# When a two-block transformer kernel takes the result tiles of its seven-product pairs and asks its residual back

## The chip, the cores and the metric

The kernel runs on one core of a Trainium2 chip. The metric is the device time of one execution in microseconds (us); the time of a kernel is the median of its runs.

## The reference

Two transformer blocks run one after the other on 512 tokens of width 1024, in float32. The change touches only the two feed-forward parts (FFNs) of the second block, which are the same code with other weights:

```
def swiglu(h, w_gate, w_up, w_down):
    return (jax.nn.silu(h @ w_gate) * (h @ w_up)) @ w_down
...
x = x + 0.5 * swiglu(rms_norm(x, ffn1_norm), ffn1_w_gate, ffn1_w_up, ffn1_w_down)
x = x + hybrid_mixer(x, ...)
x = x + 0.5 * swiglu(rms_norm(x, ffn2_norm), ffn2_w_gate, ffn2_w_up, ffn2_w_down)
return rms_norm(x, final_norm)
```

The hidden width is 2816, which is 22 pairs of 128 gate columns and 128 up columns.

## The kernel before, in words

Activations lie with the features on the 128 partitions and the 512 tokens along the free dimension; the residual is eight such tiles, `x[0]` to `x[7]`. Every float32 product is made of three fast passes: each operand is split into a rounded high part and the remaining low part, and the kernel multiplies high by high, high by low and low by high. For weights, a tile `raw` lands by DMA, ScalarE casts it to `whi` (line 364, `copy`), and VectorE subtracts to get `wlo` (line 374, `tt`). There are six buffers each for `raw`, `whi` and `wlo`, so a cast waits until TensorE has done with an earlier tile.

One FFN is the function `swiglu`. Its 22 pairs are made in three parts of 4, 9 and 9 (`PARTS`). After each part, the down product of that part's pairs is added into the residual: four groups, each for two residual tiles, with `d_evac` adding each finished accumulator into `x` on VectorE (line 370, `stt`). The four pairs of the first part are plain products on `xgh`/`xgl`. The 18 pairs of the other two parts are made with seven products of half size in place of eight (`CHAINS`, in the order p1, p5, u, p2, v, c12, c21). They need combinations of the normalized input, the forms: tiles `b1`, `b2`, `c` and `d`, made by `make_forms` on VectorE for four slices `kk` and split into `fh` (ScalarE) and `fl` (VectorE). The first chain, p1, reads `b11` for kk 0 to 3, then p5 reads `t1`, u reads `t2` (from `c`), and so on.

When the seven products of a pair are done, `seven_evac` hands the pair to a background generator, `seven_end`: Silu of the gate tile `e` on ScalarE (line 360, `act`), two multiplies on VectorE with the up tile, then the split into `hidh` (ScalarE) and `hidl` (VectorE, line 370). The down product reads `hidh` and `hidl`; a pair whose tiles are not yet made is waited for by `hidget`.

All these activation tiles come from one pool of 61 slots (`SLOTS`, function `T2`). The residual does not fit there all the time. So `first` (before part one) and `away` (after parts one and two) store the eight tiles in DRAM (`xs_f1`, `xs_f2`), and `back` loads them again: before the change in one go of eight loads, in part one ahead of the first down group, in the other parts ahead of the last pair. All loads and stores are issued by one queue, SP, in program order.

The order on each engine is fixed when the program is built. The main loop `run_units` writes TensorE's products out, and after every few of them calls `beside`, which may add one weight step and then polls the background lanes (class `Lanes`). A lane may take its next step only if `room(lane)` says that slots are left (for a lane that has begun: at most `SLOTS - 2` in use), if a planner (`Plan`) with a cost for each instruction thinks the inputs ready, and if it thinks VectorE and ScalarE not too far behind TensorE. A step that isn't allowed stays where it is until a later poll, or until the product that needs it forces it. Engines run their own rows strictly in that order.

Of the kernel before, what the change touches and what calls it, by code (L numbers as in the profile page):

```python
# [146 lines left out]
def bare(a):  # L147
    return a.ap if isinstance(a, View) else a
# [93 lines left out]
def tile_two_blocks(  # L242
# [43 lines left out]
    def committed():  # L286
        return live[0] + sum(max(0, bg.lanes[i][0][1] - bg.lanes[i][0][2][0]) for i in bg.want)

    def room(lane):
        if lane in bg.want:  # L290
            return live[0] <= SLOTS - 2
        return committed() + bg.lanes[lane][0][1] <= SLOTS - SPARE
# [7 lines left out]
    bg = Lanes(plan, len(SLACK), banks_free, room)  # L300

    def T2(name, shape=(P, T), dt=F32):
        return View(t2p.tile(list(shape), dt, name=name, tag="t2"), Token(live, bg.owner))
# [58 lines left out]
    def copy(out, in_):  # L362
        plan.op("ACT", 130.0 + width(out) / 1.2, [out], [in_])
        nc.scalar.copy(bare(out), bare(in_))  # L364
# [7 lines left out]
    def tt(out, in0, in1, op):  # L372
        plan.op("DVE", 100.0 + width(out) * 1.04, [out], [in0, in1])
        nc.vector.tensor_tensor(out=bare(out), in0=bare(in0), in1=bare(in1), op=op)  # L374
# [39 lines left out]
    def load(out, in_):  # L414
        n = 1
        for d in out.shape:
            n *= d
        plan.op("DMA", n * 4 / 360.0, [out], [], wait=2000.0)
        nc.sync.dma_start(out=bare(out), in_=bare(in_))
# [38 lines left out]
    def pair(name):  # L458
        return T2(name + "h", dt=F32R), T2(name + "l", dt=F32R)
# [5 lines left out]
    def split(src, name):  # L465
        hi, lo = pair(name)
        split_to(hi, lo, src)
        return hi, lo
# [65 lines left out]
    def add_group(*a, **k):  # L534

        g = Group(*a, **k)
        base = state["total"]
        count = len(g.pairs)
        t = 0.0
        if g.kind == "kout":  # L540
            for k in range(g.kt):
                units.append({"g": g, "k0": k, "kn": KU, "need": base + t})
                t += KU * 1360.0
            state["total"] = base + t
            return g
        if g.kind == "seven":
            for part, at in enumerate((0.0, 1.0, 3.0, 5.0)):
                units.append({"g": g, "pi": 0, "part": part, "kn": KU, "need": base + at * SEVENTH})
            state["total"] = base + 7.0 * SEVENTH
            return g  # L550
        for k0 in range(0, g.kt, g.ku):
            kn = min(g.ku, g.kt - k0)
            for pi in range(count):
                need = {
                    "feat": t + (pi * 1360.0 if count > 1 else 0.0),
                    "tok": k0 * 680.0,
                    "half": (2 * pi * g.kt + k0) * 360.0,
                    "halfin": (k0 * count + pi * kn) * 720.0,
                }[g.kind]
                units.append({"g": g, "pi": pi, "k0": k0, "kn": kn, "need": base + need})  # L560
            t += kn * count * (2720.0 if g.kind == "tok" else 1360.0)
        state["total"] = base + t
        return g
# [240 lines left out]
    x = [None] * 8  # L804
# [349 lines left out]
    hid = {}  # L1154
# [17 lines left out]
    xget = lambda k, cs=None: xg[k]  # L1172
# [16 lines left out]
    for hf in range(2):  # L1189
        i0 = 12 * hf  # L1190
        for i in range(i0, i0 + 12):
            if i == 0:
                add_group([ffn_up[0], ffn_up[1]], 8, h2get, up_evac(0),
                          kind="halfin")
            elif i > 1:
                add_group([ffn_up[i]], 8, h2get, up_evac(i), post=h.clear if i == 23 else None)
        for pp in range(4):
            add_group([ffn_down[pp][:, i0:i0 + 12, :]], 12, lambda k, cs=None, i0=i0: hid[i0 + k], dn_evac(pp, hf == 1),
                      post=hid.clear if pp == 3 else None)
# [8 lines left out]
    def drop(name, tiles):  # L1208
        rn.pop(name, None)
        tiles.clear()  # L1210

    def rnorm(name):
        bg.until(lambda: name in rn)
        return rn[name]
# [42 lines left out]
    def swiglu(wgu, wd, hidden, rname, gname, pre, d_last):  # L1257
        def gu_evac(i0):
            def ev(pi, j, ps):
                i = i0 + pi  # L1260
                r = rnorm(rname)
                if j == 0:
                    t = T2("sg")
                    tt(t, ps, r, ALU.mult)
                    act(t, t, AF.Silu)
                    tt(t, t, r, ALU.mult)
                    half[i] = t
                else:
                    t = half.pop(i)
                    tt(t, t, ps, ALU.mult)  # L1270
                    hidden[i] = split(t, "hid")
            return ev

        def seven_evac(i):
            got = {}
            L, R = slice(0, HALF), slice(HALF, T)

            def ev(what, ps):
                if what == "p1":
                    got["e"] = T2("e")  # L1280
                    copy(got["e"][:, L], ps)
                elif what == "p5":
                    got["o"] = T2("o")
                    copy(got["o"][:, R], ps)
                elif what == "u":
                    copy(got["e"][:, R], ps)
                elif what == "p2":
                    e = got["e"]
                    tt(e[:, L], ps, e[:, L], ALU.add)
                elif what == "v":  # L1290
                    copy(got["o"][:, L], ps)
                elif what == "c12":
                    e, o = got["e"], got["o"]
                    tt(e[:, R], ps, e[:, R], ALU.add)
                    tt(o[:, R], o[:, L], o[:, R], ALU.add)
                else:
                    bg.add(seven_end(i, got.pop("e"), got.pop("o"), ps), 0, 2)
            return ev

        def seven_end(i, e, o, ps):  # L1300
            L, R = slice(0, HALF), slice(HALF, T)
            yield (e,), 0
            act(e, e, AF.Silu)
            yield (e,), 0
            tt(e[:, R], e[:, R], o[:, R], ALU.mult)
            yield (e, ps), 0
            tt(e[:, L], e[:, L], ps, ALU.mult)
            del ps, o
            yield (e,), 0
            hi, lo = pair("hid")  # L1310
            act(hi, e, AF.Copy, scale=-1.0)
            yield (hi,), 0
            stt(lo, e, -1.0, hi.bitcast(F32), ALU.mult, ALU.subtract)
            hidden[i] = hi, lo

        def d_evac(pp, last):
            def ev(pi, j, ps, cs=ALL):
                if j is not None:
                    m = 2 * pp + j
                    stt(x[m][:, cs], ps[:, cs], 0.5, x[m][:, cs], ALU.mult, ALU.add)  # L1320
                if last:
                    d_last(pp, j, cs)
            return ev

        saved = {}

        def save():
            xd = saved["x"] = dram.tile([8, P, T], F32, name="xs_" + rname)
            for f in range(8):
                store(xd[f], x[f])  # L1330

        def first():
            save()
            pre()
            bg.add(make_forms(gname, rname, dict(enumerate(x))), 4, 6)
            x[:] = [None] * 8

        def back():
            for f in range(8):
                x[f] = T2("x")  # L1340
                load(x[f], saved["x"][f])

        def away():
            hidden.clear()
            save()
            x[:] = [None] * 8

        def plain_done():
            bg.until(lambda: "r" in forms)
            drop(rname, xg)  # L1350

        def hidget(i0):
            def get(k, cs=None):
                bg.until(lambda: i0 + k in hidden)
                return hidden[i0 + k]
            return get

        i0 = 0
        for n in PARTS:
            last = i0 + n == 22  # L1360
            if i0 == 0:
                add_group([wgu[0], wgu[1]], 8, xget, gu_evac(0), pre=first)
                for i in range(2, n):
                    add_group([wgu[i]], 8, xget, gu_evac(i), post=plain_done if i == n - 1 else None)
            else:
                for i in range(i0, i0 + n):
                    add_group([wgu[i]], 8, formget, seven_evac(i), kind="seven", pre=back if i == i0 + n - 1 else None,
                              post=forms.clear if i == 21 else None)
            for pp in range(4):
                kind = "half" if (last and pp == 3 and rname == "f2") else "feat"  # L1370
                post = None if pp < 3 else hidden.clear if last else away
                add_group([wd[pp][:, i0:i0 + n, :]], n, hidget(i0), d_evac(pp, last), kind=kind,
                          pre=back if i0 == 0 and pp == 0 else None, post=post)
            i0 += n

    def f1_pre():
# [347 lines left out]
    for what in MIX_ORDER.split():  # L1724
        b, evac = pieces[what[0]]
        pp = int(what[1])
# [282 lines left out]
```

## Time and profile before

| | |
|---|---|
| time, median of 3 runs | 1889.35 us (1888.68 to 1891.15) |
| the profiled execution | 1887.91 us, of which the span of the trace is 1886.1 us |
| TensorE busy | 1850.1 us, 98% of the span |
| VectorE busy | 1288.6 us, 68% |
| ScalarE busy | 961.3 us, 51% |
| chain of work that ended last | TensorE 91%, VectorE 5%, ScalarE 2%, DMA 1% |
| mean granted TensorE clock | 0.995 of full speed |

PE is TensorE, PEld its weight load (which runs beside PE), DVE is VectorE, ACT is ScalarE, SPq the queue of SP that issues DMAs. In a timeline, a row is: start in us from the span's start, duration in us, engine, line and operation, output<-input, partitions x elements, how many instructions were merged; in brackets, how long the engine had been idle before and what ended that. A matmul's duration is its time in the pipeline, so the pace of TensorE is read from the starts. In a table of stretches, a row is: the stretch, its length, the busy us of PE, PEld, DVE, ACT and POOL (instructions in brackets), the granted TensorE clock (1.00 is 2.4 GHz, 0.50 is 1.2 GHz), the DMA engines' share and GB/s. Buffer numbers are left out of names in the trace.

### The profile page before, as it was taken

To read this page: it belongs to the slowest core of one execution; us is meant where nothing else is said; L and a number is where in the kernel's file an instruction comes from. 1 tells how busy PE (TensorE), PEld (TensorE's weight loads), DVE (VectorE), ACT (ScalarE), POOL (GpSimd) and SP (SyncE) were. 2 spreads that over 40 slices of the span, in tenths; PEclk is the share of its full clock that TensorE was granted. 3 is DMA by queue.
4 is the path that set the end of the run, shared out by engine and by line. 5 is a ranking of instruction groups with operands and counts; after the bars stand their busy time and mean duration, and the time that the engine had idled before them with its cause. 6 is when DMAs were issued, how large, how long until landed. Compare 5 with 4: busy or idle time off the path is not lost.

```text
span 1886.1 us, 25909 instructions
## 1 busy us (share of the span) xinstructions
PE 1850.1 (98%) x10046; PEld 1571.5 (83%) x10046; DVE 1288.6 (68%) x2120; ACT 961.3 (51%) x1512; POOL 28.0 (1%) x53
## 2 busy tenths in 40 slices
PE   9999999999999999999999999999999999999997
PEld 6878777789888888888997998788777788988996
DVE  8799876656764466558883784677845778955864
ACT  6778686635442244343552463454576443542552
POOL 0000000000000000000000000211000000000000
PEclk9999999999999999999999999999999999999999
DMA  9665521241333323343343335321223234353341
GB/s 355 202 209 166 165 82 66 80 139 53 112 111 104 97 89 102 100 136 101 123 128 130 125 115 175 134 90 56 80 68 123 80 121 166 94 177 102 111 157 45
DMA packets 90880, 229.55 MB, mean 122 GB/s; under 512 B 10754, under 2 KB 23170, under 8 KB 90756
## 3 DMA queue, kind: packets, MB, share of 16 engines
q1 hardware_dynamic: 90756, 227.89, 36.7%
q8 instruction: 79, 1.29, 0.3%
q14 instruction: 45, 0.37, 0.1%
HBM read 211.07 MB, written 16.78 MB: 121 GB/s over the span
## 4 chain that ended last, share of the span: by engine, by line
PE 91%; DVE 5%; ACT 2%; DMA 1%; issue 1%; SPq 0%; DVEq 0%; POOLq 0%; ACTq 0%
PE acc L328 83%; PE z L328 1%; PE av L328 1%; PE pt L337 1%; DVE wlo L374 1%; DVE x L370 1%; DVE cc L370 1%; ACT whi L364 0%; DMA x<-in_xT_dram 0%; PE pd L328 0%; PE hms L328 0%; PE pg L328 0%; PE nms L328 0%; PE pe L328 0%; PE psr L328 0%
## 5 line engine op out<-in xcount | busy, mean ns | idle before, releaser
L374 DVE TENSOR_TENSOR wlo<-raw,whi 128x1024 fp32r<-128x1024 f32 (+2 forms) x396 | 445.2, 1140 | 204.7 <-ACT whi L364 201.6
L364 ACT CAST whi<-raw 128x1024 fp32r<-128x1024 f32 (+2 forms) x396 | 386.2, 985 | 325.3 <-PE acc L328 237.9
L328 PE MATMUL acc<-hh,whi 128*128 128x512 f32 (+1 forms) x800 | 298.7, 385 | 1.4 <-ACT hh L360 1.4
L328 PE MATMUL acc<-hl,whi 128*128 128x512 f32 (+1 forms) x800 | 295.6, 381 | 0.2 <-DVE hl L370 0.2
L328 PE MATMUL acc<-hh,wlo 128*128 128x512 f32 (+1 forms) x800 | 295.7, 381 | 0.0
L328 PE MATMUL acc<-fl,whi 128*128 128x256 f32 x1008 | 286.2, 284 | 4.5 <-DVE fl L374 4.5
L328 PE MATMUL acc<-fh,whi 128*128 128x256 f32 x1008 | 286.1, 284 | 0.4 <-ACT fh L364 0.4
L328 PE MATMUL acc<-fh,wlo 128*128 128x256 f32 x1008 | 285.9, 284 | 0.0
L328 PE MATMUL acc<-hidh,whi 128*128 128x512 f32 (+1 forms) x562 | 216.7, 386 | 7.9 <-ACT hidh L360 7.1
L328 PE MATMUL acc<-hidl,whi 128*128 128x512 f32 (+1 forms) x562 | 216.6, 385 | 0.9 <-DVE hidl L370 0.4
L328 PE MATMUL acc<-hidh,wlo 128*128 128x512 f32 (+1 forms) x562 | 216.1, 385 | 0.0
L328 PEld LDWEIGHTS acc<-fl,whi 128*128 128x128 f32 x1008 | 194.3, 193 | 5.0 <-DVE fl L374 4.9
L328 PEld LDWEIGHTS acc<-fh,whi 128*128 128x128 f32 x1008 | 194.2, 193 | 0.8 <-ACT fh L364 0.6
L328 PEld LDWEIGHTS acc<-fh,wlo 128*128 128x128 f32 x1008 | 194.2, 193 | 0.0
L328 PEld LDWEIGHTS acc<-hh,whi 128*128 128x128 f32 x800 | 150.3, 188 | 32.6 <-issue 2.3
L328 PEld LDWEIGHTS acc<-hh,wlo 128*128 128x128 f32 x800 | 150.4, 188 | 29.0
L328 PEld LDWEIGHTS acc<-hl,whi 128*128 128x128 f32 x800 | 150.6, 188 | 28.1 <-DVE hl L370 0.4
L328 PE MATMUL acc<-xgh,whi 128*128 128x512 f32 x352 | 142.9, 406 | 1.8 <-DVE x L370 1.8
L328 PE MATMUL acc<-xgh,wlo 128*128 128x512 f32 x352 | 137.4, 390 | 0.0
L328 PE MATMUL acc<-xgl,whi 128*128 128x512 f32 x352 | 137.2, 390 | 0.0
L328 PEld LDWEIGHTS acc<-hidh,whi 128*128 128x128 f32 x562 | 106.4, 189 | 30.2 <-ACT hidh L360 8.0
L328 PEld LDWEIGHTS acc<-hidl,whi 128*128 128x128 f32 x562 | 106.4, 189 | 22.6 <-DVE hidl L370 1.1
(301 smaller groups left out, 2679.0 us busy)
## 6 DMA issues: line engine op xcount, KB each, us to landing
raw<-in_w_in_dram SPq DMA_DIRECT2D x68, 512.0 KB, 4.2
adt<-in_ada_wT_dram SPq DMA_DIRECT2D x96, 256.0 KB, 5.5
raw<-in_ffn_up_dram SPq DMA_DIRECT2D x48, 512.0 KB, 3.8
raw<-in_f1gu_dram SPq DMA_DIRECT2D x44, 512.0 KB, 3.8
raw<-in_f2gu_dram SPq DMA_DIRECT2D x44, 512.0 KB, 3.8
raw<-in_ffn_down_dram SPq DMA_DIRECT2D x24, 512.0 KB, 4.3
xs_f<-x SPq DMA_DIRECT2D x48, 256.0 KB, 4.6
x<-xs_f SPq DMA_DIRECT2D x48, 256.0 KB, 5.6
```

Source lines behind the costliest of these rows:

```text
L328: nc.tensor.matmul(bare(out), bare(w), bare(x), start=start, stop=stop, **kw)
L337: nc.tensor.transpose(bare(out), bare(in_), idt)
L364: nc.scalar.copy(bare(out), bare(in_))
L370: nc.vector.scalar_tensor_tensor(out=bare(out), in0=bare(in0), scalar=bare(scalar), in1=bare(in1), op0=op0, op1=op1, **kw)
L374: nc.vector.tensor_tensor(out=bare(out), in0=bare(in0), in1=bare(in1), op=op)
```

## The change

Three edits. `seven_evac` takes the two result tiles `hi` and `lo` when it hands the pair over, and `seven_end` no longer asks for any: it is added with a need of 0, and `room` lets a lane whose generator needs 0 pass always. `back` takes the tiles to load: in parts two and three, `x[0]` to `x[3]` are loaded ahead of the last pair, as all eight were, and `x[4]` to `x[7]` ahead of the first down group. In part one, all eight are now loaded ahead of the last gate/up pair, one pair earlier than before.

```
--- before.py
+++ after.py
@@ -287,6 +287,8 @@
         return live[0] + sum(max(0, bg.lanes[i][0][1] - bg.lanes[i][0][2][0]) for i in bg.want)
 
     def room(lane):
+        if bg.lanes[lane][0][1] == 0:
+            return True
         if lane in bg.want:
             return live[0] <= SLOTS - 2
         return committed() + bg.lanes[lane][0][1] <= SLOTS - SPARE
@@ -1294,10 +1296,10 @@
                     tt(e[:, R], ps, e[:, R], ALU.add)
                     tt(o[:, R], o[:, L], o[:, R], ALU.add)
                 else:
-                    bg.add(seven_end(i, got.pop("e"), got.pop("o"), ps), 0, 2)
+                    bg.add(seven_end(i, got.pop("e"), got.pop("o"), ps, *pair("hid")), 0, 0)
             return ev
 
-        def seven_end(i, e, o, ps):
+        def seven_end(i, e, o, ps, hi, lo):
             L, R = slice(0, HALF), slice(HALF, T)
             yield (e,), 0
             act(e, e, AF.Silu)
@@ -1307,7 +1309,6 @@
             tt(e[:, L], e[:, L], ps, ALU.mult)
             del ps, o
             yield (e,), 0
-            hi, lo = pair("hid")
             act(hi, e, AF.Copy, scale=-1.0)
             yield (hi,), 0
             stt(lo, e, -1.0, hi.bitcast(F32), ALU.mult, ALU.subtract)
@@ -1335,10 +1336,12 @@
             bg.add(make_forms(gname, rname, dict(enumerate(x))), 4, 6)
             x[:] = [None] * 8
 
-        def back():
-            for f in range(8):
-                x[f] = T2("x")
-                load(x[f], saved["x"][f])
+        def back(fs):
+            def pre():
+                for f in fs:
+                    x[f] = T2("x")
+                    load(x[f], saved["x"][f])
+            return pre
 
         def away():
             hidden.clear()
@@ -1361,16 +1364,17 @@
             if i0 == 0:
                 add_group([wgu[0], wgu[1]], 8, xget, gu_evac(0), pre=first)
                 for i in range(2, n):
-                    add_group([wgu[i]], 8, xget, gu_evac(i), post=plain_done if i == n - 1 else None)
+                    end = i == n - 1
+                    add_group([wgu[i]], 8, xget, gu_evac(i), pre=back(range(8)) if end else None, post=plain_done if end else None)
             else:
                 for i in range(i0, i0 + n):
-                    add_group([wgu[i]], 8, formget, seven_evac(i), kind="seven", pre=back if i == i0 + n - 1 else None,
+                    add_group([wgu[i]], 8, formget, seven_evac(i), kind="seven", pre=back(range(4)) if i == i0 + n - 1 else None,
                               post=forms.clear if i == 21 else None)
             for pp in range(4):
                 kind = "half" if (last and pp == 3 and rname == "f2") else "feat"
                 post = None if pp < 3 else hidden.clear if last else away
                 add_group([wd[pp][:, i0:i0 + n, :]], n, hidget(i0), d_evac(pp, last), kind=kind,
-                          pre=back if i0 == 0 and pp == 0 else None, post=post)
+                          pre=back(range(4, 8)) if i0 and pp == 0 else None, post=post)
             i0 += n
 
     def f1_pre():
```

No instruction is added or removed in either FFN; TensorE's rows are the same in the same order. What moves stands in the same way in both FFNs at the end of part two, and in slightly different ways at the start of it. Line numbers above 290 are two higher after the change.

ScalarE, first FFN, end of part two: the last pair's gate tile is `e_8451` before and `e_8445` after; `raw_8417` and `raw_8463` before (`raw_8419` and `raw_8457` after) are the weight tiles of the third down group. Before:

```order
L364 COPY o_8471<-acc_8437 128x256
L364 CAST whi_8524<-raw_8318 128x1024
L364 CAST whi_8540<-raw_8371 128x1024
L364 CAST whi_8558<-raw_8407 128x256
L364 CAST whi_8594<-raw_8417 128x1024
L364 CAST whi_8624<-raw_8463 128x1024
L360 ACTIVATE e_8451<-e_8451 128x512
L360 ACTIVATE hidh_8632<-e_8451 128x512
```

After the change:

```order
L366 COPY o_8465<-acc_8431 128x256
L366 CAST whi_8516<-raw_8320 128x1024
L366 CAST whi_8532<-raw_8371 128x1024
L366 CAST whi_8552<-raw_8407 128x256
L362 ACTIVATE e_8445<-e_8445 128x512
L362 ACTIVATE hidh_8550<-e_8445 128x512
L366 CAST whi_8601<-raw_8419 128x1024
L366 CAST whi_8631<-raw_8457 128x1024
```

The Silu and the cast that makes `hidh` have moved ahead of two weight casts. On VectorE the two multiplies and the subtraction that makes `hidl` move ahead of the two matching `wlo` rows in the same way.

VectorE, first FFN, the last rows before the first seven-product pair reads the forms of its last slice (`b1_7245`, `b2_7246`, `c_7247`, `d_7143` before; `b1_7231`, `b2_7232`, `c_7233`, `d_7159` after). `x_...<-acc` is a residual tile that takes up a down product, `raw<-raw` are the sums of weights that the seven products need. Before:

```order
L370 SCALAR_TENSOR_TENSOR x_7203<-acc_7332,x_7203 128x512
L374 TENSOR_TENSOR c_7247<-b2_7246,b1_7245 128x256
L374 TENSOR_TENSOR b1_7245<-b1_7245 128x256
L370 SCALAR_TENSOR_TENSOR c_7247<-b1_7245,b2_7246 128x256
L370 SCALAR_TENSOR_TENSOR d_7143<-c_7247,b2_7246 128x256
L370 SCALAR_TENSOR_TENSOR x_7205<-acc_7346,x_7205 128x512
L374 TENSOR_TENSOR wlo_7366<-raw_7168,whi_7364 128x1024
L374 TENSOR_TENSOR wlo_7388<-raw_7190,whi_7386 128x1024
L374 TENSOR_TENSOR fl_7395<-b1_7245,fh_7393 128x512
L374 TENSOR_TENSOR fl_7405<-b2_7246,fh_7397 128x512
L374 TENSOR_TENSOR fl_7424<-c_7247,fh_7407 128x512
L374 TENSOR_TENSOR fl_7443<-d_7143,fh_7426 128x512
```

After the change, the making of `c` and `d` stands some 20 rows further up, with that of `b1` and `b2`:

```order
L372 SCALAR_TENSOR_TENSOR b1_7231<-x_3621,vec_78,nr_6855 128x512
L372 SCALAR_TENSOR_TENSOR b2_7232<-x_3629,vec_78,nr_6855 128x512
L376 TENSOR_TENSOR c_7233<-b2_7232,b1_7231 128x256
L376 TENSOR_TENSOR b1_7231<-b1_7231 128x256
L372 SCALAR_TENSOR_TENSOR c_7233<-b1_7231,b2_7232 128x256
L372 SCALAR_TENSOR_TENSOR d_7159<-c_7233,b2_7232 128x256
L372 SCALAR_TENSOR_TENSOR x_7100<-acc_7225,x_7100 128x512
```

and where the rows of before stood, there are now:

```order
L376 TENSOR_TENSOR fl_7341<-b1_7231,fh_7336 128x512
L376 TENSOR_TENSOR raw_7206<-raw_7184,raw_7293 128x4x128
L376 TENSOR_TENSOR raw_7206<-raw_7184 128x4x128
L376 TENSOR_TENSOR raw_7184<-raw_7206,raw_7184 128x4x128
L376 TENSOR_TENSOR raw_7302<-raw_7184,raw_7293 128x4x128
L372 SCALAR_TENSOR_TENSOR x_7110<-acc_7332,x_7110 128x512
L376 TENSOR_TENSOR fl_7366<-b2_7232,fh_7343 128x512
L372 SCALAR_TENSOR_TENSOR x_7112<-acc_7356,x_7112 128x512
L376 TENSOR_TENSOR wlo_7376<-raw_7184,whi_7374 128x1024
L376 TENSOR_TENSOR wlo_7398<-raw_7206,whi_7396 128x1024
L376 TENSOR_TENSOR fl_7424<-c_7233,fh_7368 128x512
L376 TENSOR_TENSOR fl_7443<-d_7159,fh_7426 128x512
```

The making of `c` and `d` has moved up, to before the second residual tile; `fl` of `b1` and `b2` has moved ahead of the two `wlo` rows; `fl` of `c` and `d` still stands behind them.

VectorE, second FFN, the same place. Before:

```order
L370 SCALAR_TENSOR_TENSOR x_13656<-acc_13789,x_13656 128x512
L370 SCALAR_TENSOR_TENSOR x_13658<-acc_13803,x_13658 128x512
L374 TENSOR_TENSOR wlo_13821<-raw_13615,whi_13819 128x1024
L374 TENSOR_TENSOR wlo_13843<-raw_13643,whi_13841 128x1024
L374 TENSOR_TENSOR fl_13848<-b1_13711,fh_13813 128x512
L374 TENSOR_TENSOR fl_13858<-b2_13712,fh_13850 128x512
L374 TENSOR_TENSOR fl_13877<-c_13713,fh_13860 128x512
L374 TENSOR_TENSOR fl_13896<-d_13587,fh_13879 128x512
```

After the change:

```order
L372 SCALAR_TENSOR_TENSOR x_13566<-acc_13754,x_13566 128x512
L376 TENSOR_TENSOR fl_13770<-b1_13700,fh_13764 128x512
L376 TENSOR_TENSOR fl_13778<-b2_13701,fh_13772 128x512
L376 TENSOR_TENSOR wlo_13785<-raw_13536,whi_13748 128x4x128
L376 TENSOR_TENSOR fl_13791<-c_13702,fh_13780 128x512
L372 SCALAR_TENSOR_TENSOR x_13568<-acc_13774,x_13568 128x512
L376 TENSOR_TENSOR fl_13803<-d_13603,fh_13793 128x512
L376 TENSOR_TENSOR raw_13659<-raw_13631,raw_13709 128x4x128
```

Three of the four `fl` of the last slice have moved to before the last three residual tiles, the fourth to before the last two; all now stand before the sums of weights. On ScalarE the matching `fh` casts move up as well, in both FFNs.

On SP, the eight reloads of part one now stand ahead of one weight tile that stood ahead of them. In parts two and three, four reloads stand where eight stood; the other four stand three weight tiles later, ahead of the last two weight tiles of the down product.

## Rows read from the trace of the kernel before

**Rows 1.** Stretches of 20 us; columns as told under the profile.
```profile
900.00:920.00 20.00, 17.57 (x132) 17.17 (x131) 13.86 (x21) 10.35 (x19) 0.00 (x0) 0.91 0.34 117
...
1000.00:1020.00 20.00, 16.22 (x63) 12.69 (x63) 6.22 (x9) 4.72 (x6) 0.00 (x0) 0.91 0.25 82
...
1140.00:1160.00 20.00, 20.00 (x92) 16.59 (x91) 10.57 (x15) 7.42 (x11) 0.00 (x0) 1.00 0.43 146
...
1580.00:1600.00 20.00, 17.54 (x130) 16.59 (x129) 15.64 (x23) 9.52 (x15) 0.00 (x0) 1.00 0.33 107
...
1680.00:1700.00 20.00, 16.22 (x64) 12.76 (x63) 5.52 (x8) 3.66 (x5) 0.00 (x0) 0.91 0.39 138
```

**Rows 2.** Timeline of TensorE, first FFN, down product after the second part.
```profile
1000.05 0.39 PE L328 MATMUL acc<-hidh,whi 128*128 128x512 f32 x1
...
1005.26 0.39 PE L328 MATMUL acc<-hidh,wlo 128*128 128x512 f32 x1
...
1009.21 0.50 PE L328 MATMUL acc<-hidh,whi 128*128 128x512 f32 x1 [3.56 <-ACT hidh L360]
...
1013.92 0.39 PE L328 MATMUL acc<-hidh,wlo 128*128 128x512 f32 x1
```

**Rows 3.** Timeline of ScalarE, same place.
```profile
994.66 0.41 ACT L364 CAST whi<-raw 128x256 fp32r<-128x256 f32 x1 [0.39 <-DMA x<-xs_f]
...
1005.46 1.04 ACT L364 CAST whi<-raw 128x1024 fp32r<-128x1024 f32 x1 [4.38 <-PE acc L328]
...
1006.41 0.62 ACT L360 ACTIVATE e<-e 128x512 f32<-128x512 f32 x1
```

**Rows 4.** Timeline of VectorE, same place.
```profile
994.01 2.69 DVE L374 TENSOR_TENSOR wlo<-raw,whi 128x1024 fp32r<-128x1024 f32 x3
```

**Rows 5.** One stretch of 1 us, same place.
```profile
1011.00:1012.00 1.00, 1.00 (x4) 0.79 (x3) 0.52 (x1) 0.32 (x1) 0.00 (x0) 0.50 0.01 4
```

**Rows 6.** Timeline of ScalarE, first FFN, end of the third part.
```profile
1140.63 0.63 ACT L360 ACTIVATE e<-e 128x512 f32<-128x512 f32 x1
```

**Rows 7.** Timeline of TensorE, second FFN, down product after the second part.
```profile
1688.30 0.39 PE L328 MATMUL acc<-hidh,wlo 128*128 128x512 f32 x1
...
1696.49 0.40 PE L328 MATMUL acc<-hidh,whi 128*128 128x512 f32 x1
```

**Rows 8.** Timeline of TensorE, first FFN, first seven-product pair.
```profile
899.43 0.28 PE L328 MATMUL acc<-fh,whi 128*128 128x256 f32 x1
...
900.38 0.28 PE L328 MATMUL acc<-fh,wlo 128*128 128x256 f32 x1
...
901.08 0.38 PE L328 MATMUL acc<-fh,whi 128*128 128x256 f32 x1 [0.42 <-ACT fh L364]
...
903.48 0.39 PE L328 MATMUL acc<-fl,whi 128*128 128x256 f32 x1 [2.02 <-DVE fl L374]
...
908.07 0.28 PE L328 MATMUL acc<-fh,wlo 128*128 128x256 f32 x1
```

**Rows 9.** Timeline of VectorE, first FFN, before and in that pair.
```profile
880.78 0.68 DVE L370 SCALAR_TENSOR_TENSOR x<-acc,x 128x512 f32<-128x512 f32 x1
...
900.47 2.35 DVE L374 TENSOR_TENSOR wlo<-raw,whi 128x1024 fp32r<-128x1024 f32 x2
...
902.74 1.29 DVE L374 TENSOR_TENSOR fl<-b,fh 128x512 fp32r<-128x512 f32 x2
```

**Rows 10.** Timeline of TensorE, second FFN, first seven-product pair.
```profile
1585.26 0.28 PE L328 MATMUL acc<-fh,whi 128*128 128x256 f32 x1
...
1588.00 0.39 PE L328 MATMUL acc<-fl,whi 128*128 128x256 f32 x1 [2.46 <-DVE fl L374]
```

**Rows 11.** Timeline of SP's queue, first FFN, reloads and weight tiles.
```profile
861.95 6.79 SPq L419 DMA_DIRECT2D x<-xs_f  x8
...
990.45 6.75 SPq L419 DMA_DIRECT2D raw<-in_f1d_dram  x5
```

**Rows 12.** Page, DMA issues, median us to landing last.
```profile
x<-xs_f SPq DMA_DIRECT2D x48, 256.0 KB, 5.6
```

More of the change, by code (lines that the diff above doesn't have):

```diff
@@ L289, in room @@
     def room(lane):
+        if bg.lanes[lane][0][1] == 0:
+            return True
         if lane in bg.want:
@@ L1296, in ev, with seven_end @@
                 else:
-                    bg.add(seven_end(i, got.pop("e"), got.pop("o"), ps), 0, 2)
+                    bg.add(seven_end(i, got.pop("e"), got.pop("o"), ps, *pair("hid")), 0, 0)
             return ev
-        def seven_end(i, e, o, ps):
+        def seven_end(i, e, o, ps, hi, lo):
             L, R = slice(0, HALF), slice(HALF, T)
@@ L1309, in seven_end @@
             yield (e,), 0
-            hi, lo = pair("hid")
             act(hi, e, AF.Copy, scale=-1.0)
@@ L1336, in first, with back, pre @@
             x[:] = [None] * 8
[L1338 to L1341, printed above, removed]
+        def back(fs):
+            def pre():
+                for f in fs:
+                    x[f] = T2("x")
+                    load(x[f], saved["x"][f])
+            return pre
         def away():
@@ L1363, in swiglu @@
                 for i in range(2, n):
-                    add_group([wgu[i]], 8, xget, gu_evac(i), post=plain_done if i == n - 1 else None)
+                    end = i == n - 1
+                    add_group([wgu[i]], 8, xget, gu_evac(i), pre=back(range(8)) if end else None, post=plain_done if end else None)
             else:
                 for i in range(i0, i0 + n):
-                    add_group([wgu[i]], 8, formget, seven_evac(i), kind="seven", pre=back if i == i0 + n - 1 else None,
+                    add_group([wgu[i]], 8, formget, seven_evac(i), kind="seven", pre=back(range(4)) if i == i0 + n - 1 else None,
                               post=forms.clear if i == 21 else None)
@@ L1372, in swiglu @@
                 add_group([wd[pp][:, i0:i0 + n, :]], n, hidget(i0), d_evac(pp, last), kind=kind,
-                          pre=back if i0 == 0 and pp == 0 else None, post=post)
+                          pre=back(range(4, 8)) if i0 and pp == 0 else None, post=post)
             i0 += n
```

## The prediction

> **What bounds the kernel now.** The engine shares, in the table above, say that TensorE is busy for 98% of the span, and the chain of waits ends on TensorE for 91% of it. So what a change that leaves TensorE's rows as they are can win is what TensorE loses: time in which it waits, and time in which it runs slowly. I read the table of stretches next, to find the 20 us in which TensorE is not full. Around the two feed-forward parts four stretches stand out, with 17.57, 16.22, 17.54 and 16.22 us busy, and in three of them the granted clock is 0.91 [rows 1]. Then I read the timelines of the three engines there. There are two kinds of gap, and each stands once in each FFN.
>
> **Gap B: the last pair of part two.** With all well, one matmul starts every 0.227 us: 23 of them lie between 1000.05 and 1005.26. The next should start at 1005.49 and starts at 1009.21, having waited for `hidh` [rows 2]. ScalarE's timeline says why. The Silu that begins the last pair's tail starts at 1006.41, straight behind a weight cast that had itself waited 4.38 us for TensorE [rows 3]. The order shows that cast (of `raw_8463`) ahead of the Silu. The down product that begins here has four groups of 54 matmuls; the one at 1005.26 is its 48th, so it began at 1005.26 - 47 x 0.227 = 994.6, and that cast's tile is wanted only by its 133rd, at 994.6 + 132 x 0.227 = 1024.6. In words: TensorE gives a weight buffer free, the cast runs, and only then may the Silu run for which TensorE is already waiting. Behind the gap comes a slow run: in the stretch from 1011 the clock is at 0.50, which is 1.2 GHz, though TensorE is busy all through [rows 5]. Pace is back at 1013.92, the twelfth matmul after 1005.26 [rows 2]. The loss is 8.66 - 12 x 0.227 = 5.94 us. In the second FFN ten matmuls take from 1688.30 to 1696.49 [rows 7]: 8.19 - 10 x 0.227 = 5.92 us.
>
> **Gap A: the first seven-product pair.** Eight matmuls of half size take from 899.43 to 900.38, 0.119 us each. Then the forms of the last slice are late: TensorE waits 0.42 us for `fh` and 2.02 us for `fl` [rows 8]. VectorE makes that `fl` only at 902.74, behind two weight subtractions of 2.35 us [rows 9]. Pace is back at 908.07, 27 matmuls after 900.38 [rows 8]: 7.69 - 27 x 0.119 = 4.48 us lost. In the second FFN the wait is 2.46 us, between 1585.26 and 1588.00 [rows 10], and the clock stays at 1.00 [rows 1]: 2.74 - 0.12 = 2.62 us lost.
>
> **The change part by part.** Nothing is added or removed; 48 reloads of 256 KB stay 48 [rows 12]. What counts is what stands ahead of what.
>
> *Result tiles taken early, need 0.* In the order, the Silu, the multiplies and the `hidh` cast of part two's last pair now stand ahead of the two weight casts of the third group. The Silu can start when the cast before it is done, 994.66 + 0.41 = 995.07 [rows 3]. The multiplies follow VectorE's three weight subtractions, which end at 994.01 + 2.69 = 996.70 [rows 4]. With two short multiplies, a cast and a subtraction, estimated at 2.5 us from the same steps' rows at 1006.41 to 1009.21 [rows 2, 3], `hidh` and `hidl` are ready by about 999.5. TensorE asks at 1005.49, so 6 us are to spare. Part three is a twin that already runs this way: its Silu starts at 1140.63 without a weight cast in between [rows 6], and the stretch around it has TensorE busy for 20.00 us of 20 [rows 1]. Gap B goes wholly in both FFNs: 5.94 + 5.92 = 11.86 us. The two weight casts that now come later are not late: both wait for TensorE to give a buffer free in any case, the second until 1005.46 [rows 3], 19 us before its tile is wanted.
>
> *Part one reloaded one pair earlier.* The order shows what this does to the forms. In the second FFN all four `fl` of the last slice now stand ahead of the sums of weights and of the last two residual tiles, so they are done before the products start; gap A there goes wholly, 2.62 us. In the first FFN `fl` of `b1` and `b2` move ahead of the two weight subtractions, and `fl` of `c` takes the place that the first `fl` has now: start at 902.74, done half of 1.29 us later, at 903.39 [rows 9]. TensorE wants it for the 26th matmul after 900.38, at 900.38 + 26 x 0.119 = 903.47 [rows 8]. That is level, so I leave 0 to 0.3 us of gap, take 0.1, and count 4.48 - 0.1 = 4.38 us.
>
> What stands later for it: VectorE takes up the second residual tile behind eight form rows (six in the second FFN). At no more than 0.7 us each, as the full-width row at 880.78 has it, it is done by 880.78 + 10 x 0.7 = 887.8 [rows 9]. The down product there has eight accumulators of 12 matmuls, 2.72 us each, and ends at 899.43; the sixth, which needs this tile's buffer again, starts at 899.43 - 3 x 2.72 = 891.3. So it is hidden; without that cover it would cost what it is later, some 4 us once in each FFN.
>
> *SP's queue.* In part one, eight loads that take 6.79 us to issue [rows 11] now precede one weight tile. They stand ahead of the last gate/up pair of 48 matmuls, which by the pace starts at 899.43 - (96 + 48) x 0.227 = 866.7, and what held their slots is over by about then. Begun at 866.7, the last is issued at 873.5 and, with 5.6 us to land [rows 12], there at 879.1, before VectorE first uses one at 880.78 [rows 9]. The displaced weight tile belongs to the second seven-product pair, which begins after 908. In parts two and three, four loads slip behind three weight tiles. Five weight tiles issue from 990.45 within 6.75 us [rows 11], so these loads issue before 998 and land by 1004; the group that uses them ends 2.5 x 12.3 us after the down product's start. Both cost nothing.
>
> **The sum.** 11.86 + 2.62 + 4.38 = 18.9 us off the profiled execution's 1887.91 gives 1869.0. The median of the runs before is 1889.35, 1.4 above that execution, so I expect a median of **1870.5 us**.
>
> **A rule against it.** Of the 18.9 us, the low clock holds 3 x 20 x (1 - 0.91) = 5.4 [rows 1]. Gap A of 2.46 us in the second FFN has no low clock behind it, while that of 2.44 us in the first has [rows 8, 10, 1], so the low clock is not simply bought with a gap. The Trainium skill, in "TensorE: Matmul & The Clock Gate", section "What's actually happening", says that the monitor's window runs freely, so that where the clock changes differs between runs of one kernel. By that, 5.4 us would not be safe; the two unlike A gaps agree with it. I keep them in the sum, since each low stretch follows straight on a gap that goes.
>
> **The rivals.**
>
> *The low clock comes back* behind smaller gaps that stay, such as the short ones for `hidh` and `hidl` at each FFN's first down product. For it: the unlike A gaps. Against: no low clock follows those gaps now. Time: 1870.5 + 5.4 = 1875.9.
>
> *Gap A is only half cured* in the first FFN, since the wanted `fl` is level with TensorE: 1 to 2 us of wait and 1.8 us of low clock stay. Time about 1873.8. With all of both A gaps left, 7.0 us, it would be 1877.5.
>
> *SP becomes the bound, and the kernel slower.* The second four reloads stand ahead of the last two weight tiles of each block of down products. If the pool of 61 slots were full there, SP would stand still with those tiles behind it. The first of those is wanted after 3 x 54 + 24 = 186 matmuls, at 994.6 + 186 x 0.227 = 1036.8. Less 5.6 us to land (the reloads' median, [rows 12]), 1.0 to cast [rows 3] and 1.2 to subtract [rows 9], it must issue by 1029. There are four such places, so if each were held for 18.9 / 4 = 4.7 us longer, until 1033.7, the gain would be eaten; held until 1035, the kernel would lose 4 x 6 - 18.9 = 5.1 us: 1894.5. Against: the slots that they take were given up by rows that stand before the down product's start.
>
> *It makes no difference:* the products find another wait in the same place, a weight tile for instance. Time 1889. Against: those tiles are subtracted by 996.70 [rows 4].
>
> **How the numbers follow.** The forecast (1868 to 1873) has 0.74, the low clock's return 0.10, a half cured or whole gap A 0.10, no difference 0.03, slower 0.03. The range from 1868 to 1876 takes in the first two and most of the third. About 0.2%, 3.8 us, is what a measurement of this kernel can tell from no change; the first three cases lie beyond it, so faster has 0.94, same 0.03, slower 0.03.
>
> **What would show it.** In the profile after, the stretches at the four places should have TensorE at 20.00 us, or at most 0.3 less at the first, with the clock at 1.00; the wait for `hidh` from ScalarE (a gap of 3.56 us now) should be gone from TensorE's waits; the Silu of part two's last pair should follow a 128x256 cast and not a 128x1024 one. I am wrong if a gap of over 1 us stands at one of these places, if the clock is at 0.50 where TensorE never waited, or if SP's issue of the second four reloads comes after 1010.

## The result, and the profile after

| | before | after |
|---|---|---|
| median | 1889.86 us (1888.68 to 1891.15, 4 runs) | 1869.19 us (1868.23 to 1871.85, 4 runs) |
| the profiled execution | 1887.91 us | 1869.53 us, of which the span is 1867.7 us |
| mean granted TensorE clock | 0.995 | 0.998 |

The ratio is 0.9893, 95% interval 0.9876 to 0.991: the kernel is faster by 20.7 us in the medians (17 to 23 by the interval) and by 18.4 in the profiled executions. The forecast was 1870.5.

Part 1 of the page after, busy us and share of the span: TensorE is at 99%, the other engines do the same work as before.

```profile
PE 1844.2 (99%) x10046; PEld 1567.8 (84%) x10046; DVE 1288.0 (69%) x2120; ACT 961.3 (51%) x1512; POOL 28.3 (2%) x53
```

The table of stretches after, at the places of the four stretches of [rows 1] with a gap; in the second FFN the same work now lies in the stretch before. All four have TensorE busy for 20.00 us at clock 1.00, where 16.22 to 17.57 us stood.

```profile
900.00:920.00 20.00, 20.00 (x167) 19.89 (x166) 16.89 (x26) 10.64 (x19) 0.00 (x0) 1.00 0.40 135
...
1000.00:1020.00 20.00, 20.00 (x90) 16.55 (x89) 8.55 (x12) 3.98 (x5) 0.00 (x0) 1.00 0.23 78
...
1560.00:1580.00 20.00, 20.00 (x112) 17.50 (x111) 16.86 (x26) 6.57 (x11) 0.00 (x0) 1.00 0.50 167
...
1660.00:1680.00 20.00, 20.00 (x111) 17.44 (x110) 10.07 (x16) 7.30 (x12) 0.00 (x0) 1.00 0.62 215
```

TensorE's timeline after, the same matmuls as the ends of [rows 8], [rows 2] and [rows 7] (matmuls are counted off in both traces, which have 10046 each). The first three rows are gap A of the first FFN, the next two gap B there, the last two gap B of the second FFN.

```profile
900.35 0.28 PE L330 MATMUL acc<-fh,whi 128*128 128x256 f32 x1
...
904.42 0.38 PE L330 MATMUL acc<-fl,whi 128*128 128x256 f32 x1
904.64 0.28 PE L330 MATMUL acc<-fh,wlo 128*128 128x256 f32 x1
...
996.62 0.39 PE L330 MATMUL acc<-hidh,whi 128*128 128x512 f32 x1
...
1004.55 0.39 PE L330 MATMUL acc<-hidh,wlo 128*128 128x512 f32 x1
...
1675.87 0.39 PE L330 MATMUL acc<-hidh,wlo 128*128 128x512 f32 x1
...
1678.14 0.39 PE L330 MATMUL acc<-hidh,whi 128*128 128x512 f32 x1
```

Gap A: 4.29 us from the first to the last (35 matmuls on), where before it was 908.07 - 899.43 = 8.64, so 4.35 saved. All that is left is one `fl` at 904.42, which takes 0.22 to the next start where the pace is 0.12: 0.10 us. Gap B: 7.93 (35 matmuls here too) against 1013.92 - 1000.05 = 13.87, 5.94 saved; in the second FFN 2.27 against 8.19, 5.92 saved. Gap A of the second FFN saved 2.72 by the same count (29 matmuls, 3.48 against 6.20). That is 18.93; the start of the program was 0.90 slower in this execution and the mixer 0.37 faster, which gives 18.40 of the 18.38.

ScalarE's timeline after, at the last pair of part two, which answers to [rows 3]. The Silu follows the 128x256 cast at once, and the 128x1024 cast that it stood behind now comes after `hidh`.

```profile
988.74 2.10 ACT L366 CAST whi<-raw 128x1024 fp32r<-128x1024 f32 x2
991.23 0.41 ACT L366 CAST whi<-raw 128x256 fp32r<-128x256 f32 x1 [0.39 <-PE acc L330]
991.54 0.63 ACT L362 ACTIVATE e<-e 128x512 f32<-128x512 f32 x1
994.03 0.63 ACT L362 ACTIVATE hidh<-e 128x512 fp32r<-128x512 f32 x1 [1.86 <-DVE e L376]
996.59 1.05 ACT L366 CAST whi<-raw 128x1024 fp32r<-128x1024 f32 x1 [1.93 <-PE acc L330]
```

SP's queue after, first FFN: the reload of part one, and the second four of part two.

```profile
860.07 4.17 SPq L421 DMA_DIRECT2D x<-xs_f  x8
864.64 17.56 SPq L421 DMA_DIRECT2D raw<-in_f1gu_dram  x2
...
992.21 1.85 SPq L421 DMA_DIRECT2D x<-xs_f  x4
994.15 0.86 SPq L421 DMA_DIRECT2D raw<-in_f1d_dram  x2
```

TensorE's waits after (us in total, times, longest). `hidh` from line 362 (the Silu tail's cast, 360 before) and `fl` are gone. What stays in the FFNs is the short wait for `hidh` from line 366, at part one's down product.

```profile
PE pc L330 <- DMA c_sb<-in_c_row_dram: 2.2, 1, 2.2
PE acc L330 <- DVE x L372: 1.8, 2, 1.6
PE nms L330 <- ACT nsq L362: 1.7, 1, 1.7
...
PE acc L330 <- ACT hidh L366: 0.9, 2, 0.5
```

### The profile page after: what moved, and what is told of

Its sections match the earlier page's. It is cut to its first block, busy times and chain, and to the rows that moved or that the text cites. A ratio compares the mean times of both kernels' runs of the same rounds, so it can differ in the third digit from the quotient of the medians.

```text
span 1867.7 us, 25937 instructions
## 1 busy us (share of the span) xinstructions
PE 1844.2 (99%) x10046; PEld 1567.8 (84%) x10046; DVE 1288.0 (69%) x2120; ACT 961.3 (51%) x1512; POOL 28.3 (2%) x53
## 3 DMA queue, kind: packets, MB, share of 16 engines
q8 instruction: 79, 1.29, 0.3%
## 4 chain that ended last, share of the span: by engine, by line
PE 92%; DVE 4%; ACT 2%; DMA 1%; issue 1%; SPq 0%; DVEq 0%; POOL 0%; ACTq 0%; POOLq 0%
PE acc L330 85%; PE z L330 1%; PE av L330 1%; PE pt L339 1%; DVE cc L372 1%; DVE wlo L376 0%; DVE x L372 0%; ACT whi L366 0%; PE pd L330 0%; PE hms L330 0%; PE pg L330 0%; DMA vec<-in_vecs_dram 0%; PE nms L330 0%; PE pe L330 0%; PE psr L330 0%
```

## The experiments

The time is as forecast, but the change has three edits, and for gap B the prediction named one of them as the cause from an order in which all three stand. So each part was run alone. When the program is built, the reason for gap B can be counted: the lane of the tail, not yet begun, asked 17 times in each FFN while 57 slots (56 in the second FFN) were in use, eight of them by the reloaded residual, and was refused each time until the down product forced it. A generator that needs two more is let in only up to `SLOTS - SPARE` = 57. In part three the same lane is refused once and let in at its next ask, with 29 slots in use (28 in the second FFN), since the forms are cleared there after the last pair; that is why the prediction's twin has no gap. The theory from that: what keeps the tail out is the admission rule together with eight early reloads, and curing either is enough. The theory for gap A: the planner, which sets VectorE's order, believed the reloaded tiles late.

### The tail let in, nothing else (e1) and the reload in two steps, nothing else (e2)

```
e1:  def room(lane):
+        if bg.lanes[lane][0][1] == 0:
+            return True
...
-                    bg.add(seven_end(i, got.pop("e"), got.pop("o"), ps), 0, 2)
+                    bg.add(seven_end(i, got.pop("e"), got.pop("o"), ps), 0, 0)
e2: -  pre=back if i == i0 + n - 1 else None       (ahead of the last seven-product pair)
    +  pre=back(range(4)) if i == i0 + n - 1 else None
    -  pre=back if i0 == 0 and pp == 0 else None   (ahead of the first down group)
    +  pre=None if pp else back(range(4, 8) if i0 else range(8))
```

> The kernel before with the admission rule alone: a generator that asks for no slots is always let in, and the tail of a seven-product pair is added with need 0, but still takes its result tiles late, and all reloads stay where they were. In the order, ScalarE and VectorE at the last pair of part two read as they do in the changed kernel, and at the first seven-product pair as before. Theory (gap B, the wait for hidh in part two's last pair, comes from the tail not being let in while eight reloaded tiles hold slots): gap B goes in both FFNs, 5.9 us each, gap A stays at 4.5 and 2.6, so 1889.9 - 11.9 = 1878.0, 1876 to 1880. Rival (it takes the tiles taken early, or the reload in two steps): no change, 1889 to 1891, and hidh waits 3.5 us as before.

> The kernel before with the reload in two steps of four in parts two and three alone; the tail and the admission rule are untouched, and part one reloads as before. Theory (four fewer slots held when the last pair's tail asks to be let in, so it is let in without any new rule): gap B goes in both FFNs as in the run with the admission rule alone, 1878.0, 1876 to 1880, and the two runs agree within 0.1%. Rival (my prediction's step: the tail's need and its tiles are what moves the Silu): gap B stays, 1889 to 1891.

Measured: e1 1877.61 us (ratio 0.9931, 0.9915 to 0.9948), e2 1877.70 (0.9933, 0.9918 to 0.9948), before on the same chip 1889.79. Both lose gap B whole: the 35 matmuls of gap B take 7.93 us in each, as in the changed kernel. Either edit is enough alone. With four reloads less, the lane of the tail in e2 finds 53 slots in use at its first ask and is let in. In e1's stretches, the first FFN's gap B is gone and its gap A stands as in [rows 1]:

```profile
900.00:920.00 20.00, 17.57 (x131) 17.17 (x130) 14.27 (x22) 10.33 (x18) 0.00 (x0) 0.91 0.37 117
...
1000.00:1020.00 20.00, 20.00 (x90) 16.57 (x89) 5.86 (x7) 5.01 (x6) 0.00 (x0) 1.00 0.27 90
```

### The result tiles taken early, without the admission rule (e9)

```
-                    bg.add(seven_end(i, got.pop("e"), got.pop("o"), ps), 0, 2)
+                    bg.add(seven_end(i, got.pop("e"), got.pop("o"), ps, *pair("hid")), 0, 0)
-        def seven_end(i, e, o, ps):
+        def seven_end(i, e, o, ps, hi, lo):
...
-            hi, lo = pair("hid")
```

> The kernel before with the tail's edit without its admission rule: the tail takes its two result tiles when it is added and asks for none later (need 0), all reloads as before. On every engine the order is that of the kernel before, word for word. Theory (the tiles taken early do nothing, it is the admission that counts): 1890.2, ratio 0.998 to 1.002, hidh waits 3.6 us in each FFN as before. Rival (my prediction's wording, tiles early and need 0 move the Silu): 1878.

Measured: 1889.92 us, ratio 1.0001 (0.9992 to 1.001). The part of the change that its name speaks of first does nothing by itself. Its waits of TensorE are those of the kernel before:

```profile
PE acc L328 <- ACT hidh L360: 7.1, 2, 3.6
PE acc L328 <- DVE fl L374: 4.5, 2, 2.5
```

and ScalarE's timeline has the Silu where it was, behind the cast that waits 4.38 us for TensorE:

```profile
1005.83 1.04 ACT L364 CAST whi<-raw 128x1024 fp32r<-128x1024 f32 x1 [4.38 <-PE acc L328]
1006.78 0.62 ACT L360 ACTIVATE e<-e 128x512 f32<-128x512 f32 x1
```

### All eight reloads late (e10)

```
-                    ... pre=back if i == i0 + n - 1 else None,
+                    ... pre=None,
-                          pre=back if i0 == 0 and pp == 0 else None, post=post)
+                          pre=None if pp else back(range(8)), post=post)
```

> The kernel before with all eight reloads of parts two and three asked for only when the first down group starts, none a pair ahead; part one as before. In the order ScalarE and VectorE read at the last pair as in the changed kernel. Theory (slots held by reloads kept the tail out; the loads themselves have time to spare): gap B goes, gap A stays, 1878, 1876.5 to 1880, as with four and four. Rival (my prediction's slower case: loads behind the weight tiles, SP holds them, the first accumulators wait for x): TensorE waits for DMA in the down products of parts two and three, 1880 to 1895.

Measured: 1877.31 us (0.9934, 0.9918 to 0.9951), as with four and four. Among TensorE's waits the only one that ends on a DMA is that at the program's start (2.3 us here, 2.2 to 2.5 in the other kernels). SP's queue in the first FFN:

```profile
995.51 3.82 SPq L419 DMA_DIRECT2D x<-xs_f  x8
```

The down product begins at 994.45 there, so not even eight loads behind its start are late. SP issues them in 3.82 us: the prediction's slower case, loads that hold SP because the pool is full, did not arise, and what it would cost no run shows.

### Part one's reload earlier (e3), and where it was, with the planner told that it is free (e4)

```
e3: -  add_group([wgu[i]], 8, xget, gu_evac(i), post=...)
    +  add_group([wgu[i]], 8, xget, gu_evac(i), pre=back(range(8)) if end else None, post=...)
    ...
    -  pre=back if i0 == 0 and pp == 0 else None   (ahead of the first down group)
    +  pre=None
e4:    def back():
           for f in range(8):
               x[f] = T2("x")
    +          t = plan.free["DMA"]
               load(x[f], saved["x"][f])
    +          plan.free["DMA"] = t
    +          plan.ready.pop(x[f].name, None)
```

> The kernel before with part one's eight reloads asked for one gate/up pair earlier, and nothing else. Theory (the forms of the last slice go ahead of other VectorE work): gap A goes, 4.4 us in the first FFN and 2.6 in the second, gap B stays at 5.9 each with its half clock; 1889.9 - 7.0 = 1882.9, 1881.5 to 1884. Rival (the earlier loads give back elsewhere, or the low clock returns at another place): 1885 to 1890.

> The kernel before with its reloads issued exactly where they were, but the planner that writes the engines' order is told that part one's reloads, and the others, cost no DMA time and are there at once. In the order VectorE and ScalarE read as in the run with part one's reload earlier, SP as before. Theory (gap A came from the planner's belief that the reloaded tiles arrive late, so that it put the forms behind other work, not from their arrival): gap A goes, 1882.9, 1881.5 to 1884, as in the run with the earlier reload. Rival (the tiles really arrive late): VectorE waits for DMA at the residual sums ahead of the forms, and gap A stays or grows, 1889 or more.

Measured: e3 1881.24 us, e4 1881.33 (both 0.9937 to 0.9966), a little below the range given. In both traces gap A is gone (35 matmuls in 4.27 us, 29 in 3.48 in the second FFN, where there were 6.20) and gap B stays. The 35 of the first FFN begin and end so in e4:

```profile
899.66 0.28 PE L328 MATMUL acc<-fh,whi 128*128 128x256 f32 x1
...
903.92 0.28 PE L328 MATMUL acc<-fh,wlo 128*128 128x256 f32 x1
```

SP's queue in e4 shows its eight loads issued at the time and the pace of [rows 11], which e3 issued only 3 us earlier (from 858.72, in 3.96 us):

```profile
862.19 6.78 SPq L419 DMA_DIRECT2D x<-xs_f  x8
```

That the loads cause gap A by landing late falls with this row: with the same loads at the same time, the gap goes when the planner no longer counts them. When the kernel before is built, the planner takes the eight tiles to be there 7.7 to 12.8 us after the down product's start. On the chip SP had issued all eight by 861.95 + 6.79 = 868.74 [rows 11], some 9 us ahead of that start, 899.43 - 96 x 0.227 = 877.6.

### The changed kernel without its edit to the tail (e5), and the changed kernel again (e6)

e5 keeps both moves of the reloads and takes the tail's edit back:

```
-        if bg.lanes[lane][0][1] == 0:
-            return True
...
-                    bg.add(seven_end(i, got.pop("e"), got.pop("o"), ps, *pair("hid")), 0, 0)
+                    bg.add(seven_end(i, got.pop("e"), got.pop("o"), ps), 0, 2)
...
+            hi, lo = pair("hid")
```

> The changed kernel without its edit to the seven-product pair: the tail takes its result tiles late and asks for two slots as before, the admission rule is as before; both moves of the reloads are kept. On every engine the order is the changed kernel's. Theory (the reloads do it all, the tail's edit adds nothing beside them): as the changed kernel on the same chip, 1869.2, ratio to before 0.989, the two within 0.1% of each other. Rival (the tail's edit carries gap B, as my prediction had it): hidh waits again, up to 11.9 us slower, 1881.

> The changed kernel itself, once more beside the others of this call, for the comparison within one chip: 1869.2, 1868.2 to 1871.9, ratio 0.989. In its profile no half clock but at the very end; a theory by which the clock falls at will would show one in a stretch in which TensorE never waited.

Measured on one chip: e5 1868.65 us (1868.58 to 1869.21), e6 1868.81 (1868.43 to 1870.65). Beside the two-step reload the tail's edit adds nothing; the kernel could go without it. Whether it could go without the two-step reload as well, with the tail's edit kept, was not run; e1 suggests it.

### Past both kernels: the first down product's order (e7), the forms' lane (e11), both (e8)

What is left in each FFN is part one's down product. TensorE's timeline of the changed kernel there:

```profile
879.10 0.39 PE L330 MATMUL acc<-hidh,wlo 128*128 128x512 f32 x1
880.00 0.51 PE L330 MATMUL acc<-hidh,whi 128*128 128x512 f32 x1 [0.52 <-ACT hidh L366]
880.73 0.50 PE L330 MATMUL acc<-hidl,whi 128*128 128x512 f32 x1 [0.22 <-DVE hidl L376]
881.07 0.40 PE L330 MATMUL acc<-hidh,wlo 128*128 128x512 f32 x1
```

From 879.10 to 881.07 three matmuls take 1.97 us, at pace 0.68: 1.29 us lost.

```
e7:  -  if len(order) <= 2 or k0 + kn == g.kt:
     +  if not g.wide and (len(order) <= 2 or k0 + kn == g.kt):
     ...
     +  g.wide = i0 == 0 and pp == 0
e11: -SLACK = (7000.0, 2000.0, 2000.0, 2000.0, 2000.0, ...)
     +SLACK = (7000.0, 2000.0, 2000.0, 2000.0, 3500.0, ...)
e8:  e7 and e11 together
```

> The changed kernel with one more edit: the first group of part one's down product runs over its pieces of the hidden rows first and its two output rows second, so that both wait less for the last pair's hidh and hidl (1.29 us of TensorE lost there in each FFN in the changed kernel). In the order, though, VectorE then makes fl of b1, b2 and c of the first FFN's last slice behind the first weight subtraction and that of c behind two. Theory (where the forms stand decides gap A): 2 x 1.3 us are won at the down product, and 1 to 4 us lost again at the first seven-product pair of the first FFN, so 1868 to 1871, about 1869.5. Rival (those forms are early enough all the same): 1866.6.

> As the run before it, with the planner's lane of the forms let in while VectorE is booked up to 3.5 us ahead of TensorE, not 2.0. In the order the last slice's fl of b2 and c stand ahead of the weight sums and subtractions in both FFNs, and that of d behind them. Theory (forms early and the down product's order changed, both gaps are gone): 1869.2 - 2.6 = 1866.6, 1865.5 to 1868, the fastest so far. Rival (other stages that use the same lane lose what is won, or fl of d is now late): 1869 to 1873.

> The changed kernel with the forms' lane let in while VectorE is booked up to 3.5 us ahead, and the first down product's order left alone: the other half of the fastest version. Theory (of the 3.9 us that version won, 2.5 are the down product's order and 1.4 lie in the mixer, whose generators use the same lane): 1868.8 - 1.4 = 1867.4, 1866.5 to 1868.5, and the loss of 1.3 us at the first down product stays in each FFN. Rival (the lane does no work by itself): 1868.8.

Measured: e7 1868.73 us, e8 1864.91 (1864.49 to 1865.67; ratio to before 0.9864, 0.9848 to 0.9881), beside 1868.81 for the changed kernel on that chip; e11 1869.97 (0.9899, 0.9884 to 0.9913) on another chip. e8 beats both kernels, the changed one by 3.9 us, a little more than the range given. In e7 the down product wins 1.3 us in the first FFN and 1.1 in the second, and the first gap A opens again in TensorE's timeline, as the order had it; its 35 matmuls take 6.91 us, 2.6 more than in the changed kernel:

```profile
901.66 0.39 PE L331 MATMUL acc<-fl,whi 128*128 128x256 f32 x1 [1.56 <-DVE fl L377]
...
905.43 0.39 PE L331 MATMUL acc<-fl,whi 128*128 128x256 f32 x1 [0.64 <-DVE fl L377]
```

Counted off against e6, the 3.9 us of e8 are 1.3 and 1.0 at the two down products, 0.1 at the first gap A, 0.6 ahead of the two FFNs and 0.8 in the mixer. In VectorE's timeline of e8, `fl` of `c` (its 128x512 row) precedes the two weight subtractions:

```profile
899.71 0.68 DVE L377 TENSOR_TENSOR fl<-c,fh 128x512 fp32r<-128x512 f32 x1
900.45 2.36 DVE L377 TENSOR_TENSOR wlo<-raw,whi 128x1024 fp32r<-128x1024 f32 x2
```

e11 was a miss: I expected 1.4 us of gain, and its profiled matmuls end 2.2 us later than e6's; the ratios to the kernel before (0.9899 and 0.9886) can't be told apart. Counted off against e6 it wins 0.9 us ahead of the FFNs, 0.1 at the first gap A and 0.9 in the mixer, but in the second FFN the wait for the first down product's `hidh` grows to 1.35 us, which with the slow clock behind it costs 2.6, and another slow stretch costs 1.6. In e8 that `hidh` isn't waited for, since the down product asks for it later. Alone, neither edit wins anything that can be told from no change; together they win 3.9 us.

## Why the prediction was right, point by point

- *What bounds the kernel, and the two gaps*: right. The gaps gave 18.93 us, forecast 18.9: gap B 5.94 and 5.92 (the same), gap A 4.35 (4.38) and 2.72 (2.62).
- *Gap B, the working*: the Silu was to start at 995.07 in the time of the trace before. The same matmul lies 1000.05 - 996.62 = 3.43 us earlier after, which makes it 991.64; it started at 991.54. `hidl` was to be ready at 999.5, so 996.1; VectorE's timeline has it done by 995.4.
- *Gap B, the cause*: here a step failed, the one headed "Result tiles taken early, need 0". It took what the order showed of the whole change for the work of that edit. Early tiles and need 0 without the admission rule do nothing (e9); the rule does it alone (e1), and so does the two-step reload (e2, e10), to which the prediction gave no part of the sum. In the change the two are there together, and one is spare (e5). The 11.86 us came out all the same, and not by luck: they were read from the order of the whole change, which does not show which edit made it.
- *Gap A*: right, to the tenth that was left: `fl` of `c` starts at 903.68 where it was to start at 902.74 + 0.92, and 0.10 us of gap stays (0.1 was taken). That the reload does this through the planner, not by landing earlier, the prediction left open; e4 shows it.
- *SP's queue*: harmless, as forecast, but its times were off. Part one's reload was issued from 860.07, not from 866.7: it did not have to wait for the products that I thought held its slots. The second four loads went out at 992.21 (before 998 was forecast), and e10 shows that they could come later still.
- *A rule against it*: the three slow stretches went with their gaps, as the sum had it, and none came back in the changed kernel's two profiles. But the doubt was sound: of its four executions the slowest, 1871.85 us, has a mean granted clock of 0.997 and the others 0.998, about what one slow stretch takes; and the next point shows more.
- *The low clock comes back*: in the two profiles it did not, but it does in other kernels of this study, behind gaps that none of them changed (last section). Its price, 5.4 us, was that of all three stretches, 1.8 each. Where one can be told from the gap ahead of it, it costs 1.5 to 1.6 us, so one alone gives 1872.
- *The median*: 1.3 us below the forecast. The sum was taken off a median that lay 1.4 above the profiled execution before; after, the median lies 0.3 below its profiled execution; against that, 0.5 of the 18.9 were given back at the program's start and in the mixer together. The 1.4 was no constant: it is about one slow stretch more in the usual execution before than in the profiled one (last section).

## What to carry to other kernels

Where a builder orders the engines' rows, a wait on the chip can come from a rule of the builder: ask which count refused the late step, and look at what else holds that count. When a change has several edits and the order shows only their sum, build each alone before giving one of them the gain; here two of three cure the same gap, and taking the result tiles early does nothing by itself. And a planner that overrates one transfer pays in another place, with rows that have nothing to do with that transfer.

## What the runs showed of the hardware

The granted clock falls behind some gaps and not behind others of the same size. After the first FFN TensorE waits 1.64 us for `x`, in all kernels alike. The stretches of 5 us with that gap, of e6 and then of e2, where TensorE is busy for the same 3.17 us:

```profile
1180.00:1185.00 5.00, 3.17 (x13) 2.06 (x12) 3.60 (x6) 3.13 (x5) 0.00 (x0) 1.00 0.73 232
```

```profile
1185.00:1190.00 5.00, 3.17 (x10) 2.10 (x10) 3.56 (x6) 3.31 (x5) 0.00 (x0) 0.83 0.78 242
```

The clock falls to 0.50 behind it in e2, e9, e10 and e11, and the 38 matmuls around it take 13.0 us; in before, after, e1 and e3 to e8 it stays at 1.00 and they take 11.4 to 11.5. The second FFN's gap A is the other case. Its wait is 2.46 us in the kernel before [rows 10] and also in e2, but here with the slow clock behind it:

```profile
1583.61 0.39 PE L328 MATMUL acc<-fl,whi 128*128 128x256 f32 x1 [2.46 <-DVE fl L374]
```

```profile
1580.00:1600.00 20.00, 17.54 (x134) 17.33 (x133) 13.89 (x20) 10.08 (x18) 0.00 (x0) 0.91 0.39 116
```

There 29 matmuls take 7.68 us in e2, 6.20 before: 1.48 us more for the same wait. In every trace each slow stretch but that at the program's end begins in a gap of TensorE or straight behind one; the smallest of these gaps is 1.74 us between two starts (e11), while one of 1.84 in e7 has no slow stretch behind it. Over the 13 traces the clock fell at all 8 gaps B, at 9 of the 10 gaps A that stand as before, and at 4 of the 13 waits for `x`.

The executions of one kernel differ in the same way. Of the 13 of the kernel before that ran beside e9, the one with a mean granted clock of 0.995 took 1887.71 us, the six with 0.994 took 1888.43 to 1889.48, the six with 0.993 took 1889.79 to 1891.33. The profile of before, at 0.995, has three slow stretches ahead of that at the end; the profile of e9, at 0.993 and with the same order on every engine, has five. The Trainium skill, in "TensorE: Matmul & The Clock Gate", section "What's actually happening", says that the monitor's window runs freely and does not begin anew with the kernel, so that the point at which the clock changes varies from run to run. These executions agree with that; the window itself no trace here shows.

So here a gap of 2 us cost 2 us or 3.5, and it differed between kernels that do not touch it: part of what a profile shows as gained or lost elsewhere is this. It is also part of the 20.7 us between the medians, against 18.4 between the profiled executions: a kernel without the gaps has fewer places where the clock falls.
